# Sample attention of a decoder step: keys turned in 32x32 blocks on VectorE, scores on four row groups, new tokens once for all batches

## The chip, the cores and the metric

The kernel runs on one core of one Trainium2 chip. The metric is the device time of one launch in microseconds (us); lower is better. Profiles come from one execution that the hardware profiler recorded. Engine names are those of the profile: PE is TensorE, PEld its weight load, DVE VectorE, ACT ScalarE, POOL GpSimd, SP SyncE (here an issuer of DMAs).

## The reference

One step of a hybrid decoder layer in float32: 256 prompt tokens and 8 batches of 8 sample tokens go through two token mixers in parallel (HGRN2 with 8 heads, and MLA attention with 8 heads), a gated merge, an output projection and a squared-ReLU MLP, with modulated norms in between. The model width is 2048. The part that is changed is the sample attention:

```python
def mla_sample_attention(q_lat, q_pe, ckv_new, kpe_new, cache_ckv_l, cache_kpe_l, page_table):
    ckv_past = cache_ckv_l[page_table].reshape(Bd, -1, KV_RANK)      # 8 x 1024 x 512
    kpe_past = cache_kpe_l[page_table].reshape(Bd, -1, ROPE_DIM)     # 8 x 1024 x 64
    s_past = einsum('bthc,bsc->bhts', q_lat, ckv_past) + einsum('bthr,bsr->bhts', q_pe, kpe_past)
    s_new = einsum('bthc,bsc->bhts', q_lat, ckv_new) + einsum('bthr,bsr->bhts', q_pe, kpe_new)
    s_new = where(causal, s_new, -inf)
    p = softmax(concatenate([s_past, s_new], -1) * MLA_SCALE)
    return einsum('bhts,bsc->bthc', p[..., :P], ckv_past) + einsum('bhts,bsc->bthc', p[..., P:], ckv_new)
```

Per batch there are 64 queries (8 tokens of 8 heads) with 512 + 64 features, 1024 past tokens on 8 pages of a pool, and the 8 new tokens of the batch. The cached rows are both keys and values.

## The kernel before

Most of the program is large projections, features on partitions, 320 tokens (256 + 64) as the moving columns. `gemm` takes 256 columns of a weight matrix: SP loads 8 x 128 rows of it into a `raw` tile (pool `wraw`, three of 1 MB each); ACT casts half of a tile at a time to a rounded part `whi` and DVE subtracts it for a remainder `wlo` (pool `whl`, three of each); three PE products per block then give float32 accuracy (`whi` with the high part of the tokens, `whi` with the low, `wlo` with the high). PSUM has eight banks of 512 columns: four in pool `acc`, four in pool `aux`.

The MLA mixer projects two heads at a time (`mla_proj`), does the prompt's attention for them, and leaves the absorbed sample queries in `qst`: six blocks of 128 partitions, of which four are the 512 latent features and two hold the 64 rotary features on the lower and on the upper half of the partitions. A first projection for the other mixer, `early_proj(0)`, stands behind the last pair of heads, and `early_proj(1)` behind the sample attention.

The sample attention runs over the eight batches in turn. For each:

- `gather(b)` (L735) issues three indirect DMAs on POOL: the rotary keys `kraw` and the latent rows in two halves of 512 tokens, the first into `craw` (pool `sr`, three buffers), the second into a `raw` tile of `wraw`. A partition holds eight tokens.
- `past_scores(b, hf)` (L751), once for each half: PE turns 16 blocks of 128 x 128 through PSUM, which ACT and DVE copy by turns to `th` tiles; then products of 64 queries with 512 keys, the feature blocks by turns on two column groups of PE, accumulate in one bank; `kraw` is turned and multiplied in the same way. `fold` (L727) has ACT copy one column group to `Ss2` and DVE add it to the other.
- `new_scores(b)` (L782) adds the scores against the new tokens of all batches, with a mask that leaves those of batch b.
- `softmax` (L790), on DVE and ACT, over 64 x 1088 scores.
- `turn(b-1)` (L798) turns P on PE; `values(b-1)` (L808) multiplies it with `craws` and `ckvs` (the new tokens' rows) in eight products on two column groups and a ninth; `latent(b-2)` (L818) adds the column groups and turns the result into `olat`.

`at` says behind which feature block of `past_scores(b)` the steps of the batches before it are issued. The last batch's turn, values and latent are in `sample_tail` (L847), a generator which `gemm` advances between quarters of `early_proj(1)`'s products. What follows is the value projection with `w_kv_up` on `olat` (L859 to L870). Each engine works through its own queue in order; the queue's order is made from the program by the framework's scheduler, and tiles of a pool are given to a new user when the last reader of the old one is done.

Of the kernel before, what the change touches and what calls it, by code (L numbers as in the profile page):

```python
# [18 lines left out]
NP = 256  # L19
NB = 8  # L20
# [62 lines left out]
def tile_hgrn2_mla_step(  # L83
# [68 lines left out]
    def load_w(w2d, k0, nk, c0, ncols, src=None):  # L152
        """rows k0*128.., columns c0..: hi / lo operand views per k tile"""
# [39 lines left out]
    def gemm(w2d, kt0, nkt, c0, xh, xl, fine=False):  # L193
        """[256 columns of w2d from c0].T @ x -> two banks [128, N]"""
# [18 lines left out]
    def rstd_of(x, tmp, r):  # L213
        """r = 1/sqrt(x), x already mean square plus eps"""
# [32 lines left out]
    ckvs = keep.tile([NS, RANK], F32, name="ckvs")  # L247
    xsm = x_sample.rearrange("b t d -> (b t) d")
# [4 lines left out]
    qst = mq.tile([P, 6, NB, NS], F32, name="qst")  # L253
# [47 lines left out]
    def ada_turn():  # L301
        """the last columns of the conditioning, features on partitions, with their bias"""
# [10 lines left out]
    def ada_gen():  # L313
        """the conditioning, nb blocks of 128 columns of it (mod[:, b0:b0+nb, :]) in nb steps"""
# [70 lines left out]
    part1 = dram.tile([P, 4, 2, N], F32, name="part1")  # L385

# [1 line left out]
    def partial(f0, nf, cols, outs):  # L388
        """adds the rows of features f0.. of two 256-column blocks of w_in to outs"""
# [24 lines left out]
    def partial_kpe(f0, nf):  # L414
        """the rotary key's columns, on both partition halves"""
# [54 lines left out]
    def hg_gates(qT, qr, fg, fr, tmp, hp):  # L470
        """query and forget gates of a pair of heads"""
# [103 lines left out]
    nc.gpsimd.memset(qst[64:P, 4], 0.0)  # L575
    nc.gpsimd.memset(qst[0:64, 5], 0.0)

    def early_proj(j):
        """a projection of the second pair of heads, ahead of the mixer: forget (0) or query (1)"""
        ps = gemm(w_in, 0, KF, (1024, 0)[j] + 256, hh, hl, True)  # L580
        for h in range(2):
            nc.scalar.copy(out=part[:, 4 + j, h], in_=ps[h][:, 0:N])

    with mstack, pool("mp2", 2) as mp2:
        def mla_proj(i):
# [5 lines left out]
            # absorbed weights of the sample queries  # L591
# [6 lines left out]
            # queries  # L598
# [21 lines left out]
            # keys and values  # L620
# [24 lines left out]
            # sample queries: absorbed, and rotary on both partition halves  # L645
            for m in range(2):
# [8 lines left out]
                nc.scalar.copy(out=qst[64:P, 5, :, hs], in_=v)  # L655
# [40 lines left out]

        pend = None
        for i in range(NH // 2):
# [14 lines left out]
    # sample attention over the paged cache  # L713
    ostack = ExitStack()
    olp = ostack.enter_context(pool("olp"))
    olat = olp.tile([P, RF, NH, NS], F32, name="olat")
    ckv_rows = cache_ckv[0].rearrange("n (g j) c -> (n g) (j c)", j=8)
    kpe_rows = cache_kpe[0].rearrange("n (g j) c -> (n g) (j c)", j=8)
    with pool("sr", 3) as sr, pool("sc", 2) as sc, pool("s1") as s1:

        def cp(i, out, in_):
            if i % 2:
                nc.vector.tensor_copy(out=out, in_=in_)
            else:
                nc.scalar.copy(out=out, in_=in_)

        def fold(S, psc, cs, n, mask=None):  # L727
            """adds the two column groups of the scores"""
            S2 = s1.tile([NS, 512], F32, name="Ss2")
            nc.scalar.copy(out=S2[:, 0:n], in_=psc[64:P, 0:n])  # L730
            if mask is not None:
                add(S2[:, 0:n], S2[:, 0:n], mask)
            add(S[:, cs], psc[0:64, 0:n], S2[:, 0:n])

        def gather(b):  # L735
# [13 lines left out]
            return kraw, craws  # L749

        def past_scores(b, hf, S, kraw, craw, at):  # L751
            psc = bank(acc)
            ths = []

            def scores(f):
                for g in range(2):
                    mm(psc[64 * g:64 * (g + 1)], qst[:, f + g, b], ths[f + g], f == 0, False)

            for f in range(RF):
                pt = bank()  # L760
                for j in range(4):
                    transpose(pt[:, j * P:(j + 1) * P], craw[:, j, f * P:(f + 1) * P], P)
                th = sc.tile([P, 512], F32, name="th", bufs=4)
                cp(f, th, pt)
                ths.append(th)
                if f == 2:
                    scores(0)
                if f in at:
                    at[f]()
            pt = bank()  # L770
            for j in range(2):
                transpose(pt[:, j * P:(j + 1) * P],
                          kraw[:, 4 * hf + 2 * j:4 * hf + 2 * j + 2].rearrange("p o c -> p (o c)"), P)
            kt = sc.tile([P, 2, P], F32, name="ktp")
            cp(hf, kt, pt[:, 0:256].rearrange("p (j s) -> p j s", j=2))
            scores(2)
            pv_ = psc.rearrange("p (j o s) -> p o j s", j=2, o=2)
            for g in range(2):
                mm(pv_[64 * g:64 * (g + 1), g], qst[:, 4 + g, b], kt, False, True)
            fold(S, psc, slice(hf * 512, (hf + 1) * 512), 512)  # L780
# [619 lines left out]
```

## Time and profile before

| what | before |
|---|---|
| time, median of three runs | 2184.15 us (2177.47, 2185.85, 2184.15) |
| span of the profiled execution | 2179.5 us |
| PE busy | 2126.7 us, 98% |
| DVE busy | 1076.7 us, 49% |
| ACT busy | 877.8 us, 40% |
| POOL busy | 165.7 us, 8% |
| bytes moved by DMA | 401.94 MB, mean 184 GB/s |
| mean granted PE clock | 0.995 |

The profiled execution has no time of its own beside its span, which runs from the first to the last instruction. Busy shares are means over the span; the sample attention lies at about 375 to 532 us in it. In a row of a timeline the first number is the start, the second the duration, and what stands in brackets at its end is the time the engine was idle before it and what ended that. Rows of the same kind close together are one row with a count.

### The profile page before, as it was taken

How to read it: one execution, taken by the hardware profiler on the slowest of the kernel's cores; microseconds unless marked ns; L12 is line 12 of the kernel's file. 1: busy time of each engine (PE TensorE's matmuls, PEld its weight loads, DVE VectorE, ACT ScalarE, POOL GpSimd, SP SyncE). 2: the span in 40 equal slices, each digit the busy share in tenths (PEclk: the TensorE clock that was granted, in tenths of full speed). 3: DMA queues.
4: the chain of work that ended last, by engine and by line, in shares of the span. 5: the costliest groups of instructions: out<-in, count | busy, mean ns of one | idle time of the engine just before them, and what ended most of it. 6: DMA issues, size and time to landing. Idle time of an engine off the chain costs nothing.

```text
span 2179.5 us, 34849 instructions
## 1 busy us (share of the span) xinstructions
PE 2126.7 (98%) x14716; PEld 1908.5 (88%) x14716; DVE 1076.7 (49%) x1644; ACT 877.8 (40%) x1328; POOL 165.7 (8%) x158
## 2 busy tenths in 40 slices
PE   6999999999899999999999899999999999999997
PEld 3788988457688888999999599999999999999996
DVE  3556743443865646543443643344444444444455
ACT  4432443333554445333343543434333333333353
POOL 0000001110531311000010000000000000000001
PEclk9999999999999999999999999999999999999998
DMA  8986555235577668766864555545444544454442
GB/s 253 322 297 238 163 170 198 92 131 159 169 245 242 215 220 280 226 213 196 261 227 139 193 162 187 157 153 155 147 146 153 155 146 147 153 155 145 147 151 71
DMA packets 327571, 401.94 MB, mean 184 GB/s; under 512 B 10984, under 2 KB 265528, under 8 KB 324472
## 3 DMA queue, kind: packets, MB, share of 16 engines
q1 hardware_dynamic: 301576, 363.07, 51.8%
q0 software_dynamic: 3584, 21.50, 2.8%
q10 hardware_dynamic: 22256, 15.16, 2.3%
q8 instruction: 115, 1.88, 0.4%
q14 instruction: 40, 0.33, 0.0%
HBM read 387.69 MB, written 12.01 MB: 183 GB/s over the span
## 4 chain that ended last, share of the span: by engine, by line
PE 89%; issue 4%; DVE 3%; ACT 1%; DMA 1%; POOL 1%; SPq 0%; DVEq 0%; ACTq 0%; POOLq 0%
PE acc L131 77%; PE aux L131 8%; PE aux L134 4%; DVE wlo L143 1%; DMA raw<-in_w_in_dram 1%; POOL X L137 1%; ACT whi L146 1%; DMA xt<-in_x_sample_dram 0%; DVE zu L1363 0%; DVE x L1280 0%; DVE X L143 0%; DVE zg L137 0%; POOL qt L137 0%; DVE qn L494 0%; DVE bb L913 0%
## 5 line engine op out<-in xcount | busy, mean ns | idle before, releaser
L143 DVE TENSOR_TENSOR wlo<-raw,whi 128x1024 fp32r<-128x1024 f32 (+1 forms) x493 | 602.1, 1227 | 721.2 <-ACT whi L146 721.0
L146 ACT CAST whi<-raw 128x1024 fp32r<-128x1024 f32 (+1 forms) x493 | 501.6, 1025 | 809.2 <-PE acc L131 647.9
L131 PE MATMUL acc<-hh,whi 128*128 128x320 f32 x1168 | 369.0, 317 | 3.4 <-ACT hh L146 2.3
L131 PE MATMUL acc<-hl,whi 128*128 128x320 f32 x1168 | 361.8, 310 | 0.3 <-DVE hl L143 0.3
L131 PE MATMUL acc<-hh,wlo 128*128 128x320 f32 x1168 | 360.5, 311 | 0.0
L131 PE MATMUL acc<-uh,whi 128*128 128x320 f32 x1024 | 316.6, 309 | 0.0
L131 PE MATMUL acc<-gh,whi 128*128 128x320 f32 x1024 | 316.2, 309 | 0.0
L131 PE MATMUL acc<-gh,wlo 128*128 128x320 f32 x1024 | 316.1, 309 | 0.0
L131 PE MATMUL acc<-ul,whi 128*128 128x320 f32 x1024 | 316.1, 309 | 0.0
L131 PE MATMUL acc<-uh,wlo 128*128 128x320 f32 x1024 | 316.0, 309 | 0.0
L131 PE MATMUL acc<-gl,whi 128*128 128x320 f32 x1024 | 315.9, 309 | 0.0
L131 PEld LDWEIGHTS acc<-hh,whi 128*128 128x128 f32 x1168 | 219.6, 188 | 33.7 <-issue 18.2
L131 PEld LDWEIGHTS acc<-hl,whi 128*128 128x128 f32 x1168 | 219.6, 188 | 2.9 <-DVE hl L143 1.4
L131 PEld LDWEIGHTS acc<-hh,wlo 128*128 128x128 f32 x1168 | 218.9, 188 | 3.2 <-DVE wlo L143 2.5
L131 PEld LDWEIGHTS acc<-uh,whi 128*128 128x128 f32 x1024 | 192.5, 188 | 1.7 <-ACT u L1332 0.8
L131 PEld LDWEIGHTS acc<-gh,whi 128*128 128x128 f32 x1024 | 191.9, 187 | 1.8 <-ACT u L1333 0.8
L131 PEld LDWEIGHTS acc<-ul,whi 128*128 128x128 f32 x1024 | 192.4, 188 | 0.0
L131 PEld LDWEIGHTS acc<-uh,wlo 128*128 128x128 f32 x1024 | 192.4, 188 | 0.0
L131 PEld LDWEIGHTS acc<-gh,wlo 128*128 128x128 f32 x1024 | 192.0, 187 | 0.1
L131 PEld LDWEIGHTS acc<-gl,whi 128*128 128x128 f32 x1024 | 192.0, 188 | 0.0
L131 PE MATMUL aux<-raw,cT 128*32 128x512 f32 (+1 forms) x832 | 113.7, 593 | 16.7 <-DVE tt L137 11.9
L140 POOL TENSOR_TENSOR ssum<-ssum,sqt 128x320 f32<-128x320 f32 x26 | 25.9, 997 | 981.2 <-ACT sqt L1213 966.8
(409 smaller groups left out, 2602.2 us busy)
## 6 DMA issues: line engine op xcount, KB each, us to landing
raw<-in_w_ada_dram SPq DMA_DIRECT2D x96, 1024.0 KB, 6.9
raw<-in_w_up_dram SPq DMA_DIRECT2D x64, 1024.0 KB, 5.7
raw<-in_w_down_dram SPq DMA_DIRECT2D x64, 1024.0 KB, 5.8
raw<-in_w_in_dram SPq DMA_DIRECT2D x60, 1024.0 KB, 6.2
raw<-in_w_o_dram SPq DMA_DIRECT2D x16, 1024.0 KB, 5.9
raw<-in_w_in_dram SPq DMA_DIRECT2D x20, 512.0 KB, 6.4
raw<-in_w_b_out_dram SPq DMA_DIRECT2D x8, 1024.0 KB, 6.3
raw<-in_w_a_out_dram SPq DMA_DIRECT2D x8, 1024.0 KB, 5.8
```

Of the source, the lines that this page charges most:

```text
L131: nc.tensor.matmul(out, lhsT=lhsT, rhs=rhs, start=start, stop=stop)
L134: nc.tensor.transpose(out=out, in_=in_, identity=ident[:k, :k])
L137: (eng or nc.vector).tensor_tensor(out=out, in0=a, in1=b, op=ALU.mult)
L140: (eng or nc.vector).tensor_tensor(out=out, in0=a, in1=b, op=ALU.add)
L143: return (eng or nc.vector).tensor_tensor(out=out, in0=a, in1=b, op=ALU.subtract)
L146: nc.scalar.copy(out=hi, in_=src)
```

## The change

- The keys are turned by DVE. `blocks32` is one `nc.vector.transpose` over 128 x 512 elements, which turns each 32 x 32 block in its place. A batch takes eight of them into tiles of the pool `whl` (`th` is now a `whi` or a `wlo`) and one for the rotary keys, `ktp`.
- A block of 32 keys on 32 partitions of feature block k stays on its own partition group q. Scores are products of 32 rows, 64 queries and 256 keys: 18 feature blocks of 32 for each of four partition groups, by turns on two column groups. Each partition group has a PSUM bank of its own, so that a batch takes all four banks of `acc`. `fold` becomes four copies of 64 x 256 on ACT and four adds on DVE.
- The queries are needed on all four partition groups. `sample_queries` writes them to a DRAM tensor `qdr` with 18 DMAs issued on ACT, behind the last `mla_proj`; `gather` reads a batch's queries four times into `qrep` with DMAs on SP.
- The scores against the new tokens are computed in `sample_queries` for all batches, into `snew`; `softmax` has POOL copy them into S. The scale by the sum's reciprocal moves from DVE to ACT.
- P of the new tokens is collected in `pnew`; the product with `ckvs` is done once for all batches at the end (four products and four adds in `sample_tail`). The bank of `values` comes from `aux`.
- `qst` has five blocks, and its pool closes before the attention. Comments and docstrings are left out of the file.

```diff
+        def sample_queries():
+            for bc_ in range(4):
+                for f in range(RF):
+                    nc.scalar.dma_start(out=qdr[:, :, 4 * f + bc_].rearrange("b u q -> u b q"),
+                                        in_=qst[32 * bc_:32 * (bc_ + 1), f])
+            for k in range(2):
+                nc.scalar.dma_start(out=qdr[:, :, 16 + k].rearrange("b u q -> u b q"), in_=qst[32 * k:32 * (k + 1), 4])
+            for b in range(NB):
+                psn = bank()
+                for f in range(RF):
+                    g = f % 2
+                    mm(psn[64 * g:64 * (g + 1), 0:NS], qst[:, f, b], ckvT[:, f, NP:N], f < 2, f == 3)
+                mm(psn[0:64, 0:NS], qst[:, 4, b], kpeT[:, NP:N], False, True)
+                nc.scalar.copy(out=snew[:, b], in_=psn[64:P, 0:NS])
+                add(snew[:, b], snew[:, b], cst[0:NS, C_NEW + b * NS:C_NEW + (b + 1) * NS])
+                add(snew[:, b], psn[0:64, 0:NS], snew[:, b])
...
+        sample_queries()
         early_proj(0)
...
+            qrep = sc.tile([P, 18, NS], F32, name="qrep", bufs=3)
+            for q in range(4):
+                nc.sync.dma_start(out=qrep[32 * q:32 * (q + 1)], in_=qdr[b])
+            return kraw, craws, qrep
+        def blocks32(out, src):
+            nc.vector.transpose(out=out.rearrange("p k j u -> p j k u"),
+                                in_=src.rearrange("p j (k u) -> p j k u", u=32))
+        def turn_keys(b, kraw, craws):
+            ths = []
             for f in range(RF):
-                pt = bank()
-                for j in range(4):
-                    transpose(pt[:, j * P:(j + 1) * P], craw[:, j, f * P:(f + 1) * P], P)
-                th = sc.tile([P, 512], F32, name="th", bufs=4)
-                cp(f, th, pt)
+                th = whl.tile([P, 1024], F32, name="wlo" if f % 2 else "whi").rearrange(
+                    "p (k j u) -> p k j u", k=4, j=8)
+                for hf in range(2):
+                    blocks32(th[:, :, 4 * hf:4 * hf + 4], craws[hf][:, :, f * P:(f + 1) * P])
                 ths.append(th)
+            kt = sc.tile([P, 2, 8, 32], F32, name="ktp")
+            blocks32(kt, kraw)
+            return ths, kt
+        def past_scores(b, S, ths, kt, qrep):
+            psc = [bank(acc) for _ in range(4)]
+            for k0 in range(0, 18, 2):
+                for q in range(4):
+                    qs = slice(32 * q, 32 * (q + 1))
+                    for g in range(2):
+                        k = k0 + g
+                        rhs = (ths[k // 4][qs, k % 4] if k < 16 else kt[qs, g]).rearrange("p j u -> p (j u)")
+                        mm(psc[q][64 * g:64 * (g + 1), 0:256], qrep[qs, k], rhs, k0 == 0, k0 == 16)
+            Sv = S[:, 0:PAST].rearrange("t (j q u) -> t q j u", j=8, q=4)
+            for q in range(4):
+                S2 = s1.tile([NS, 256], F32, name="Ss2", bufs=2)
+                nc.scalar.copy(out=S2, in_=psc[q][64:P, 0:256])
+                add(Sv[:, q], psc[q][0:64, 0:256].rearrange("t (j u) -> t j u", j=8),
+                    S2.rearrange("t (j u) -> t j u", j=8))
+        def softmax(b, S):
             mx = sc.tile([NS, 2], F32, name="mxs")
+            nc.gpsimd.tensor_copy(out=S[:, PAST:PAST + NS], in_=snew[:, b])
...
-            nc.vector.tensor_scalar(out=S, in0=S, scalar1=mx[:, 1:2], scalar2=None, op0=ALU.mult)
+            nc.scalar.activation(out=S, in_=S, func=AF.Copy, scale=mx[:, 1:2])
...
-            nc.vector.tensor_copy(out=PT[0:64, 8], in_=pt2[0:64, 0:64])
+            nc.vector.tensor_copy(out=pnew[:, b], in_=pt2[0:64, 0:64])
...
         def values(PT, craws):
-            po = bank(acc)
+            po = bank()
...
-            mm(po[0:64], PT[0:64, 8], ckvs, False, True)
...
         for b in range(NB):
+            kraw, craws, qrep = gather(b)
             S = sc.tile([NS, PAST + NS], F32, name="Ss")
+            ths, kt = turn_keys(b, kraw, craws)
+            past_scores(b, S, ths, kt, qrep)
+            if b > 1:
+                latent(b - 2, ot)
+            if b:
+                PT = turn(b - 1, st["S"])
+            softmax(b, S)
+            if b:
+                ot = values(PT, st["c"])
+            st["S"], st["c"] = S, craws
...
             latent(NB - 1, ot)
+            for f in range(RF):
+                pn = pns[f % 2]
+                mm(pn, ckvs[:, f * P:(f + 1) * P], pnew.rearrange("s b q -> s (b q)"), True, True)
+                ov = olat[:, f].rearrange("p h (b t) -> p b h t", t=NT)
+                add(ov, ov, pn.rearrange("p (b h t) -> p b h t", b=NB, h=NH))
```

The order of the instructions on the engines moves with it. The rows below are from the engines' queues; a number behind a name is that of the tile, and the last figures are the shape. First DVE in the middle of the attention, before the change: `th` and `ktp` are copies of turned keys, `Ss` the scores and `mxs` the softmax's maximum and sum.

```order
L795 RECIPROCAL mxs_3836<-mxs_3836 64x1
L796 TENSOR_SCALAR Ss_3713<-Ss_3713,mxs_3836 64x1088
L140 TENSOR_TENSOR Ss_3848<-acc_3849,Ss2_3895 64x512
L723 COPY th_3921<-aux_3916 128x512
L140 TENSOR_TENSOR Ss2_3904<-Ss2_3904,cst_75 64x64
L805 COPY PTs_3934<-aux_3924 64x64
L140 TENSOR_TENSOR Ss_3848<-acc_3898,Ss2_3904 64x64
L723 COPY th_3951<-aux_3946 128x512
L723 COPY ktp_3968<-aux_3965 128x256
L140 TENSOR_TENSOR Ss_3848<-acc_3908,Ss2_3974 64x512
L723 COPY th_4003<-aux_3998 128x512
L792 TENSOR_REDUCE mxs_3977<-Ss_3848 64x1
```

And the same stretch of DVE's queue now, from one batch's reciprocal on (`craw_4256` and `raw_4258` hold the keys of the batch after the one whose scores are `Ss_4113`):

```order
L803 RECIPROCAL mxs_4084<-mxs_4084 64x1
L764 STREAM_TRANSPOSE whi_4266<-craw_4256 128x4x4x32
L764 STREAM_TRANSPOSE wlo_4269<-craw_4256 128x4x4x32
L764 STREAM_TRANSPOSE whi_4272<-craw_4256 128x4x4x32
L764 STREAM_TRANSPOSE whi_4266<-raw_4258 128x4x4x32
L764 STREAM_TRANSPOSE wlo_4269<-raw_4258 128x4x4x32
L764 STREAM_TRANSPOSE whi_4272<-raw_4258 128x4x4x32
L764 STREAM_TRANSPOSE wlo_4275<-craw_4256 128x4x4x32
L764 STREAM_TRANSPOSE wlo_4275<-raw_4258 128x4x4x32
L140 TENSOR_TENSOR Ss_4113<-acc_4128,Ss2_4204 64x8x32
L140 TENSOR_TENSOR Ss_4113<-acc_4129,Ss2_4207 64x8x32
L140 TENSOR_TENSOR Ss_4113<-acc_4130,Ss2_4210 64x8x32
```

The eight turns of the next batch's keys now stand ahead of the adds of this batch's scores. On PE, at the same place, from the latent step of the batch before last (`Ss_4113` and `craw_4104` are of one batch, `whi_4418` and `qrep_4412` of the next but one):

```order
L131 MATMUL aux_4368<-cst_75,ot_4252 128x64 x4
L134 MATMUL aux_4374<-ident_76,Ss_4113 128x64 x8
L134 MATMUL aux_4375<-ident_76,Ss_4113 64x64
L131 MATMUL acc_4432<-whi_4418,qrep_4412 64x256 x2
L131 MATMUL acc_4433<-whi_4418,qrep_4412 64x256
L131 MATMUL aux_4395<-craw_4104,PTs_4385 64x512 x4
L131 MATMUL aux_4395<-raw_4106,PTs_4385 64x512 x4
L131 MATMUL acc_4433<-whi_4418,qrep_4412 64x256
```

Three score products of the batch after the next stand between the turn of a batch's P and its values. On ACT, ahead of the attention (`Sp`, `mxp`: the last prompt softmax; `whi_3551` and what follows it: `early_proj(0)`), before:

```order
L673 ACTIVATE Sp_3424,mxp_3427<-Sp_3424,mxp_3427 128x128
L675 ACTIVATE Sp_3424,mxp_3427<-Sp_3424,mxp_3427 128x256
L146 CAST whi_3526<-raw_3496 128x1024
L582 COPY part_86<-acc_3436 128x320
L582 COPY part_86<-acc_3437 128x320
```

and now:

```order
L673 ACTIVATE Sp_3417,mxp_3420<-Sp_3417,mxp_3420 128x128
L675 ACTIVATE Sp_3417,mxp_3420<-Sp_3417,mxp_3420 128x256
L701 DMA qdr_164<-qst_102 32x8x64 x11
L711 COPY snew_98<-aux_3447 64x64
L711 COPY snew_98<-aux_3456 64x64
L711 COPY snew_98<-aux_3465 64x64
L146 CAST whi_3551<-raw_3521 128x1024
L146 CAST whi_3581<-raw_3579 128x1024
L711 COPY snew_98<-aux_3474 64x64
L146 CAST whi_3609<-raw_3579 128x1024
```

Eleven DMA issues and three copies stand between the last prompt softmax and the casts of `early_proj(0)`.

More of the change, by code (lines that the diff above doesn't have):

```diff
@@ L711, in tile_hgrn2_mla_step @@
     lrstack.close()
+    qst_stack.close()
     ostack = ExitStack()
@@ L770, in past_scores @@
[L770 to L779, printed above, removed]
@@ L780, in past_scores @@
-            fold(S, psc, slice(hf * 512, (hf + 1) * 512), 512)
-        def new_scores(b, S):
-            psn = bank(acc)
-            for f in range(RF):
-                g = f % 2
-                mm(psn[64 * g:64 * (g + 1), 0:NS], qst[:, f, b], ckvT[:, f, NP:N], f < 2, f == 3)
-            mm(psn[0:64, 0:NS], qst[:, 4, b], kpeT[:, NP:N], False, True)
-            fold(S, psn, slice(PAST, PAST + NS), NS, cst[0:NS, C_NEW + b * NS:C_NEW + (b + 1) * NS])
-        def softmax(S):
+                th = whl.tile([P, 1024], F32, name="wlo" if f % 2 else "whi").rearrange(
+                    "p (k j u) -> p k j u", k=4, j=8)
```

58 lines of the change are left out of this document (12 added, 46 removed).

## The prediction

> **What bounds the kernel now.** I read the page's head first, then the windows around the sample attention, then single engines' timelines inside one batch of it.
>
> ```profile
> span 2179.5 us, 34849 instructions
> PE 2126.7 (98%) x14716; PEld 1908.5 (88%) x14716; DVE 1076.7 (49%) x1644; ACT 877.8 (40%) x1328; POOL 165.7 (8%) x158
> PE 89%; issue 4%; DVE 3%; ACT 1%; DMA 1%; POOL 1%; SPq 0%; DVEq 0%; ACTq 0%; POOLq 0%
> ```
>
> TensorE (PE) is busy 98% of the span and carries 89% of the chain that ended last. Whatever takes work off it shortens the program, unless something else then makes it wait. The windows give the stage that is changed and one batch of it (columns: PE, weight loads, DVE, ACT, POOL busy, granted clock, DMA share, GB/s):
>
> ```profile
> 374.00:532.00 158.00, 157.56 (x940) 86.84 (x941) 66.08 (x127) 57.68 (x103) 15.09 (x16) 1.00 0.36 118
> 430.00:447.70 17.70, 17.70 (x108) 9.01 (x106) 7.28 (x16) 6.46 (x12) 2.83 (x3) 1.00 0.40 134
> ```
>
> PE never idles here; DVE works 7.28 of 17.70 us. Two gathers of the POOL timeline give the period of a batch, 454.21 - 436.50 = 17.71 us, and show that a gather starts when a values product of PE lets its buffer go:
>
> ```profile
> 436.50 0.94 POOL L747 DMA_INDIRECT craw<-in_cache_ckv_dram,pidx  x1 [12.44 <-PE acc L131]
> 440.83 0.94 POOL L747 DMA_INDIRECT raw<-in_cache_ckv_dram,pidx  x1 [0.30 <-issue]
> 454.21 0.94 POOL L747 DMA_INDIRECT craw<-in_cache_ckv_dram,pidx  x1 [12.44 <-PE acc L131]
> ```
>
> Nobody waits for that gather now: its keys are wanted a whole batch later. From the PE timeline (an f32 product is two records; products in two column groups overlap):
>
> ```profile
> 434.28 1.94 PE L131 MATMUL acc<-craw,PTs 128*64 128x512 f32 x8
> 436.05 1.89 PE L131 MATMUL acc<-raw,PTs 128*64 128x512 f32 x8
> 437.87 1.07 PE L131 MATMUL acc<-ckvs,PTs 64*64 64x512 f32 x2
> 438.87 0.44 PE L134 MATMUL aux<-ident,kraw 128*128 128x128 f32 x2
> 439.24 1.08 PE L131 MATMUL acc<-th,qst 128*64 128x512 f32 x4
> 440.14 0.60 PE L131 MATMUL acc<-ktp,qst 128*64 128x256 f32 x4
> 440.68 1.09 PE L134 MATMUL aux<-ident,craw 128*128 128x128 f32 x8
> ```
>
> Values of one batch take 437.87 - 434.28 = 3.59 us, the new tokens' product on one column group 1.00, two score products of 512 columns 440.14 - 439.24 = .90. The stage runs from 374.97 to the first product of `olat`, 532.41: 157.4 us.
>
> ```profile
> 374.97 1.47 PE L134 MATMUL aux<-ident,craw 128*128 128x128 f32 x12
> 532.41 1.78 PE L131 MATMUL aux<-olat,raw 128*128 128x64 f32 x15
> ```
>
> **The change, part by part.**
>
> *PE loses work.* The 40 transposes of a batch, the new tokens' scores and the ckvs product go; 72 products of 32 rows and 256 columns replace 18 of 512. No row shows 32-row groups at work. By the .90 above a column pair of 256 costs .45, so 36 pairs cost 16.2 us if the four row groups run in turn and 4.05 if they run together. I take 4.05: each group has its own rows, its own bank and its own queries. With .7 for turning P, 1.0 for `latent` and 3.59 for values PE then needs about 9.4 us a batch where it needs 17.7: at most 8.3 us a batch to win.
>
> *DVE gains nine turns of 512 columns a batch*, and loses its half of the PSUM copies.
>
> ```profile
> 426.97 0.69 DVE L723 COPY th<-aux 128x512 f32<-128x512 f32 x1 [0.41 <-PE aux L134]
> 429.93 0.68 DVE L140 TENSOR_TENSOR Ss<-acc,Ss 64x512 f32<-64x512 f32 x1 [0.18 <-ACT Ss L730]
> 424.90 1.27 DVE L792 TENSOR_REDUCE mxs<-Ss 64x1 f32<-64x1088 f32 x1
> L143 DVE TENSOR_TENSOR kt<-bb 128x512 f32<-128x512 f32 x4 | 4.9, 1225 | 0.1
> ```
>
> A turn moves as much as the copy (.69); the dearest 512-column row is 1.225. Bounds .55 (a fifth under the copy) to 1.225; I take .70, since a turn reads one operand as the copy does. DVE's sum: 9 x .70, four adds of 256 columns at .40 (.68 halved, and something for the fixed part), reduce 1.27, small ones .9: 10.1 us a batch.
>
> [...]
>
> *A chain forms.* In DVE's order the eight turns of batch b+2 stand ahead of the adds of batch b+1. On PE three score products stand ahead of `values(b)`, and they need banks that the first two of those adds free. `values(b)` frees the buffers that gather b+3 waits for. So each period is: half of values, gather, last turns, two adds, three products, and round again; what was hidden under 17.7 us of PE work is now in series.
>
> ```profile
> raw<-in_w_in_dram SPq DMA_DIRECT2D x60, 1024.0 KB, 6.2
> raw<-in_cache_ckv_dram,pidx POOLq DMA_INDIRECT x8, 5.8
> craw<-in_cache_ckv_dram,pidx POOLq DMA_INDIRECT x8, 8.1
> ```
>
> Landings: 5.8 us for the gather of `raw` (1 MB), and 10.1 from the issue of `craw` to the landing of `raw` in the timeline above (440.83 - 436.50 + 5.8), with 4.3 of it between the issues. Issued one behind the other I estimate 5.5 for `craw` and 3.2 more for `raw` (8.7; bounds 5.8 and 10.1). Three turns fit into the 3.2; five follow. Period: 1.9 + 5.5 + 3.2 + 5 x .70 + 2 x .40 + .4 + about .7 of hand-overs = 16.0 us, against 17.71.
>
> *The clock.* PE then works 9.4 of 16 us, with its idle time in one piece of 5 to 6. What follows such a piece is seen elsewhere in this trace (clock is the third number from the end):
>
> ```profile
> 1222.00:1225.50 3.50, 1.69 (x16) 0.16 (x8) 3.46 (x7) 1.75 (x3) 0.00 (x0) 1.00 1.04 403
> 1225.50:1228.90 3.40, 1.14 (x12) 0.16 (x8) 3.40 (x4) 3.27 (x7) 0.00 (x0) 1.00 1.05 408
> 1228.90:1232.30 3.40, 1.93 (x8) 0.20 (x8) 1.57 (x6) 2.85 (x7) 0.00 (x0) 0.50 1.05 408
> 1232.30:1235.80 3.50, 3.48 (x14) 1.21 (x14) 3.44 (x15) 0.00 (x0) 0.00 (x0) 0.51 1.05 409
> ```
>
> A window with PE at 1.14 of 3.40 is followed by 3.4 us and more at .50. Here the products that come next are those on the chain, .4 + 1.9 us; at half clock they cost up to 2.3 more, and since the phase wanders I take 1.3: a period of 17.3.
>
> *Ahead of the stage.* Eighteen DMA issues on ACT write the queries out, eleven of them in a row, ahead of the copies of the new scores and of `early_proj(0)`'s casts.
>
> ```profile
> 259.28 0.54 ACTq L514 DMA_DIRECT2D out_dram<-ckvs  x1
> 259.88 0.56 ACTq L521 DMA_DIRECT2D out_dram<-ktok  x1
> 260.49 1.20 ACTq L522 DMA_DIRECT2D out_dram<-ktok  x1
> 360.00 1.04 ACT L146 CAST whi<-raw 128x1024 fp32r<-128x1024 f32 x1
> 370.12 0.31 PE L131 MATMUL acc<-hh,wlo 128*128 128x320 f32 x1
> ```
>
> At .54 to .6 an issue, 11 take some 6 us from 360.0 on, where ACT now casts; PE stands meanwhile, and 4 us of new-score products move here as well. I add 10.1 (bounds 4 and 13). Of the moved DMAs the 32 loads of `qrep` stand on SP between the two projections' weight loads; they are due a batch ahead and hidden as long as the gather is what is waited for.
>
> *The tail.* ACT and DVE have the hi and lo parts of `early_proj(1)`'s first weights ahead of the last batch's adds. Its second load waits for a lo part of the first, and the first for `values(5)`.
>
> ```profile
> 491.11 10.06 SPq L156 DMA_DIRECT2D raw<-in_w_in_dram  x2
> 507.11 1.23 DVE L143 TENSOR_TENSOR wlo<-raw,whi 128x1024 fp32r<-128x1024 f32 x1 [1.78 <-ACT whi L146]
> 512.27 0.67 DVE L140 TENSOR_TENSOR Ss<-acc,Ss 64x512 f32<-64x512 f32 x1
> ```
>
> Today's issue of the second load waits too (10.06 us) but PE has scores to do. Then: `values(5)` 3.9, load 5.8 to 6.2, cast 1.04, two lo parts 2.4, second load 6.2, cast and lo 2.3: the adds come some 7 us after their place in the period. Behind them:
>
> ```profile
> 427.46 1.20 ACT L794 ACTIVATE Ss<-Ss,mxs 64x1088 f32<-64x1088 f32 x1
> 428.56 0.19 ACT L794 ACTIVATION_READ_ACCUMULATOR Ss<-Ss,mxs 64x1 f32 x1
> 369.97 0.31 PE L131 MATMUL acc<-hl,whi 128*128 128x320 f32 x1
> ```
>
> 9.7 us to the end of the last turn (two adds .8, reduce 1.3, exponential 1.4, the scale, now on ACT over the same 1088 columns, 1.2, turn .7; the rest hand-overs, and PE on GEMM products in between), 4.4 to the values (copy of P, and a quarter of the GEMM: 24 products at 370.12 - 369.97 = .15 are 3.6), values 3.8, another quarter 3.6, `latent` 1.0, four new-token products of 512 columns 3.5, the last quarter 3.6: 29.6, and 29.8 with the hand-overs.
>
> **The sum**, in us after PE is free: adds of batches 0, 1 and 2 at 8.3, 15.3 and 31.4 (their keys have landed; DVE's twelve queued turns set the pace, then the chain); four periods of 16.0 to batch 6 at 95.5; the last adds at 95.5 + 16 + 7.5 = 119.0; end at 148.8. With the half clock: 32.5, four of 17.4 to 102.1, 126.5, end 158.6. Against 157.4 and with 10.1 ahead: +1.5 at full clock, +11.3 with the clock halved each period. I take the second, 2179.5 + 11.3 = 2190.8 for the profiled execution; on the median of the runs, 2184.15 + 11.3 = 2195.5. The profiled span lies 4.65 below that median, inside the spread 2177.47 to 2185.85. What this measurement tells from no change is about 0.5%, 10.9 us.
>
> **The rivals.**
> 1. *The chain binds, the clock holds*: +1.5, 2186. For it: windows at half load (1.69 of 3.50) are not followed by .50 above. Against: the idle piece is longer than a window.
> 2. *The gather runs ahead*, landing faster or being released earlier than I read, so that DVE's 10.1 us (with hand-overs 10.6) sets the period: (17.7 - 10.6) x 6.5 = 46 less, + 10 ahead = -36, 2148; a gather of 6 instead of 8.7 alone gives 2.7 x 7 = 19 less than my sum, 2176. For it: 118 GB/s in the stage against 403 to 409 above, so the DMAs have room. Against: one gather's own 5.8.
> [...]
> 4. *Row groups run in turn*: 16.2 + 5.3 = 21.5 us a batch on PE, 3.8 x 8 = 30 over before, and the 10 ahead and the tail's 6: 2230. For it: no row shows four groups together. Against: column pairs do overlap (two products of 512 columns in .90, one alone in 1.00).
>
> **How the numbers follow.** Main case .45: its own range, with hand-overs, phase and the ACT issues at their bounds, is 2185 to 2210, so .17 of it lies within 0.5% and .28 above. Rival 1 .18, all within. Rival 2 .20, faster. Rival 3 .09 and rival 4 .08, slower. Faster .20, same .35, slower .45. The range 2168 to 2228 leaves out the far part of rival 2 (about .12) and rival 4 with the end of 3 (.07).
>
> **What would show it.** In the changed trace: STREAM_TRANSPOSE rows of about .70; POOL's gathers 17 us apart, their wait ending on a `values` product of PE; DVE's turns waiting for DMA `raw`; PE idle 5 to 6 us a batch ahead of score products, released by DVE's adds; clock near .8 in the stage; eleven ACT issues and PE idle by 361 to 367; DVE's lo parts ahead of the last adds. The forecast is wrong if the turns wait for nothing, if PE has no long idle piece, if the four row groups' products start more than .1 us apart in a row, or if a turn is far from .70.

## The result and the profile after

The changed kernel takes 2207.07 us (median of four runs, 2205.07 to 2212.29) against 2183.64 us before (2177.47 to 2185.85): ratio 1.0104, 95% interval 1.0086 to 1.0121. It is slower by 23 us. The forecast was slower by 11.3, 2195.5, with a range of 2168 to 2228.

The head of the page after, and the line on which source lines carry the chain that ended last:

```profile
span 2206.2 us, 36328 instructions
PE 2098.0 (95%) x15380; PEld 1901.5 (86%) x15380; DVE 1098.7 (50%) x1688; ACT 866.0 (39%) x1304; POOL 168.1 (8%) x165
PE acc L131 74%; PE aux L131 10%; PE aux L134 2%; DMA raw<-in_cache_ckv_dram,pidx 2%; DMA raw<-in_w_in_dram 2%; DVE wlo L143 1%; ACT whi L146 1%; POOL X L137 1%; DVE wlo L764 0%; DVE whi L764 0%; DMA xt<-in_x_prompt_dram 0%; DVE zu L1370 0%; DVE x L1287 0%; DMA oB<-obs 0%; DVE X L143 0%
```

PE is busy for 28.7 us less and the program still got longer: the gather of `raw`, which nobody waited for, now stands on the chain with 2%, and the load of `in_w_in` with 2% instead of 1%. Three rows of PE's timeline give the borders of the stage, the first score product and the first product of `olat`, and the wait ahead of it:

```profile
367.43 0.70 PE L131 MATMUL aux<-ckvT,qst 128*64 128x64 f32 x8 [6.79 <-DVE snew L140]
386.02 1.14 PE L131 MATMUL acc<-whi,qrep 32*64 32x256 f32 x20
554.51 7.25 PE L131 MATMUL aux<-olat,raw 128*128 128x64 f32 x64
```

The stage starts 386.02 - 374.97 = 11.05 us later and takes 554.51 - 386.02 = 168.5 us instead of 157.4: 22.1 us in all. The profiled spans differ by 26.7; the 4.6 us behind the stage are no part of the change (in the profiles below, that rest of the program varies between 1647 and 1655 us).

Four periods in the windows view (columns as before: PE, PEld, DVE, ACT, POOL busy, granted clock, DMA share, GB/s):

```profile
407.00:427.40 20.40, 12.00 (x175) 6.80 (x175) 9.06 (x19) 5.30 (x11) 2.42 (x4) 0.75 0.49 146
427.40:447.80 20.40, 12.67 (x179) 6.93 (x177) 8.90 (x18) 5.00 (x10) 3.03 (x5) 0.75 0.48 146
447.80:468.20 20.40, 12.93 (x179) 6.98 (x177) 8.91 (x18) 5.23 (x10) 2.19 (x4) 0.75 0.42 133
468.20:486.70 18.50, 12.86 (x177) 6.90 (x175) 8.91 (x18) 5.03 (x10) 2.12 (x4) 0.76 0.34 115
```

No engine is busy for more than 13 of 20.4 us, where PE was busy for all of its 17.7 before; the work is in series. The clock is granted at .75. The ring can be read off three timelines. POOL's gathers, released by a values product:

```profile
427.11 0.97 POOL L755 DMA_INDIRECT craw<-in_cache_ckv_dram,pidx  x1 [2.28 <-PE aux L131]
428.83 0.94 POOL L755 DMA_INDIRECT raw<-in_cache_ckv_dram,pidx  x1 [0.75 <-PE aux L131]
...
447.58 0.97 POOL L755 DMA_INDIRECT craw<-in_cache_ckv_dram,pidx  x1 [2.30 <-PE aux L131]
```

DVE's turns, released by the landings, with the adds behind them:

```profile
433.08 0.71 DVE L764 STREAM_TRANSPOSE whi<-craw 128x512 f32<-128x512 f32 x1 [6.01 <-DMA craw<-in_cache_ckv_dram,pidx]
...
438.90 0.71 DVE L764 STREAM_TRANSPOSE whi<-raw 128x512 f32<-128x512 f32 x1 [3.92 <-DMA raw<-in_cache_ckv_dram,pidx]
...
441.91 0.71 DVE L140 TENSOR_TENSOR Ss<-acc,Ss 64x256 f32<-64x256 f32 x2
```

And PE's three products (six records) with the values behind them, released by the adds:

```profile
442.34 1.44 PE L131 MATMUL acc<-whi,qrep 32*64 32x256 f32 x6 [7.64 <-DVE Ss L140]
443.74 3.55 PE L131 MATMUL aux<-craw,PTs 128*64 128x512 f32 x8
447.12 1.88 PE L131 MATMUL aux<-raw,PTs 128*64 128x512 f32 x8
```

From gather to gather: `craw` lands 6.0 us behind its issue (427.11 to 433.08), `raw` another 5.8 later, turns 3.0, adds .4, three products 1.4, half of the values 3.4 where they took 1.8 before, and the next gather at 447.58: 20.5 us.

### The profile page after: what moved, and what is told of

Same layout as the page of the kernel before. It is cut to its first block, busy times and chain, and to the rows that moved or that the text cites. A ratio compares the mean times of both kernels' runs of the same rounds, so it can differ in the third digit from the quotient of the medians.

```text
span 2206.2 us, 36328 instructions
## 1 busy us (share of the span) xinstructions
PE 2098.0 (95%) x15380; PEld 1901.5 (86%) x15380; DVE 1098.7 (50%) x1688; ACT 866.0 (39%) x1304; POOL 168.1 (8%) x165
## 4 chain that ended last, share of the span: by engine, by line
PE 86%; DVE 5%; DMA 4%; issue 2%; ACT 2%; POOL 1%; ACTq 0%; SPq 0%; DVEq 0%; POOLq 0%
PE acc L131 74%; PE aux L131 10%; PE aux L134 2%; DMA raw<-in_cache_ckv_dram,pidx 2%; DMA raw<-in_w_in_dram 2%; DVE wlo L143 1%; ACT whi L146 1%; POOL X L137 1%; DVE wlo L764 0%; DVE whi L764 0%; DMA xt<-in_x_prompt_dram 0%; DVE zu L1370 0%; DVE x L1287 0%; DMA oB<-obs 0%; DVE X L143 0%
## 5 line engine op out<-in xcount | busy, mean ns | idle before, releaser
L131 PE MATMUL acc<-hh,whi 128*128 128x320 f32 x1168 | 370.5, 318 | 14.9 <-DVE Ss L140 11.5
L131 PEld LDWEIGHTS acc<-hh,whi 128*128 128x128 f32 x1168 | 220.2, 189 | 46.8 <-issue 19.3
```

The source lines that it names most:

```text
L131: nc.tensor.matmul(out, lhsT=lhsT, rhs=rhs, start=start, stop=stop)
```

## The experiments

Each kernel was timed against the kernel before on the same chip; its ratio stands beside the changed kernel's 1.0104. One per cent is 22 us. Code is cut down to the lines that matter, and comments in it are added here. Where a place in the profile is compared, it is the first product of `olat`, at 554.51 in the changed kernel.

### One ordering edge on TensorE

```diff
+            with behind(st.get("v")):          # the last product of values(b-2)
                 past_scores(b, S, ths, kt, qrep)
```

(`behind` queues what the block issues on an engine behind the instruction named.)

> The changed kernel with one ordering edge on TensorE: the score products of batch b+2 are queued behind the values of batch b, instead of three of them ahead. Nothing else is changed. Theory (series): values wait for DVE's adds through those three products, the adds for turns, the turns for a gather, the gather for values; 20.4 us a batch. Without the three products values(b) wait only for the softmax of b. The ring then goes over two batches: 1.9 + gather 10 + turns 3.5 + adds 1.7 + softmax 4.5 + turn of P and copy 1.4 = 23, 11.5 a batch; five to six periods shorter by 8.5 to 8.9: about 2207 - 46 = 2161, and under the kernel before. Rival (transfers): the gather and the loads of the queries share the DMA engines and set the pace, whatever the order on PE: some 2 us a batch from the earlier start, 2195. Rival (DVE): nine turns on DVE set the pace: no change, 2207.

Measured: 1.0124 (1.0094 to 1.0153): no change. The number is that of the rival on DVE, for another reason, as the run with DVE's order changed shows below. What falls is the reading that the three products alone hold the values. PE's queue, then ACT's, of this kernel say what holds them:

```profile
442.18 3.68 PE L131 MATMUL aux<-craw,PTs 128*64 128x512 f32 x8 [9.33 <-ACT PTs L817]
```

```profile
440.82 0.70 ACT L798 COPY Ss<-acc 64x256 f32<-64x256 f32 x2 [9.06 <-DVE Ss L143]
441.55 0.58 ACT L817 COPY PTs<-aux 128x512 f32<-128x512 f32 x1
```

The copy of P, `PTs`, is queued on ACT behind the third and fourth copies of the next batch's scores, and these wait 9 us for a `Ss2` buffer that DVE's adds give back. There were two links in parallel from the adds to the values, one on PE and one on ACT.

### The other link, and both

```diff
-                S2 = s1.tile([NS, 256], F32, name="Ss2", bufs=2)
+                S2 = s1.tile([NS, 256], F32, name="Ss2", bufs=4)
```

This edit alone, with TensorE's order as it was:

> The changed kernel with four Ss2 buffers instead of two, and TensorE's order as it is (three score products ahead of the values). Theory (two parallel links, each enough): the link on TensorE holds the values as before: no change, 2207 (within 6). If the link on ACT alone were what counts, it would be 2164.

Measured: 1.0095 (1.0070 to 1.0120): no change, as the theory of two links has it. In its profile `PTs` is copied at 432.95 and the values still start only at 441.14, behind three products that wait 6.80 us for an add. And with the edge on TensorE beside it:

> The changed kernel with values ahead of the score products on TensorE, and with four Ss2 buffers instead of two. The second edit is for the second link that the trace of the first showed: on ACT the copies 3 and 4 of the scores wait for a Ss2 buffer that DVE's adds free, and the copy PTs, which the values wait for, is queued behind them. With both links out, values(b) wait only for the softmax of b. Theory (series, two parallel links): the ring goes over two batches, by rows of the changed kernel: values .. gather's landing .. turns .. adds 16.7, softmax, turn of P and copy 8.5: 25 for two, 12.6 a batch instead of 20.4; five to six periods: 2207 - 43 = 2164, under the kernel before. Rival (transfers): gathers and query loads set the pace: not under 2190. Rival (DVE's order, turns ahead of adds, is itself the bound): 2205.

Measured: 1.0022 (1.0009 to 1.0036), some 18 us shorter than the changed kernel; the first product of `olat` is at 539.6. So each link alone holds the values, and it takes both edits to gain. But 43 us were expected. PE's timeline shows what still waits:

```profile
440.43 3.12 PE L131 MATMUL acc<-whi,qrep 32*64 32x256 f32 x30 [3.28 <-DVE Ss L143]
...
448.00 1.10 PE L131 MATMUL aux<-cst,ot 128*128 128x64 f32 x8
449.03 0.77 PE L134 MATMUL aux<-ident,Ss 64*128 64x64 f32 x9
450.42 1.94 PE L131 MATMUL aux<-craw,PTs 128*64 128x512 f32 x8 [0.62 <-ACT PTs L817]
```

The whole score products of the next batch wait for banks that the adds free, and the turn of P and the values are queued behind them: a third way from the adds to the values, longer by one batch's scores. That this third way is what the missing 25 us are is read from the queue; the next run tests it only by cutting all three ways at once.

### The turns behind the adds

All three ways begin at adds that stand behind turns. One edge on DVE takes that away (TensorE's order moves with it, the values ahead of the score products, which alone had gained nothing):

```diff
+            with behind(st.get("a")):          # the last add of batch b-1
                 ths, kt = turn_keys(b, kraw, craws)
```

> The changed kernel with one ordering edge on DVE: the turns of batch b+1 are queued behind the adds of batch b. (TensorE's order moves with it: the values come ahead of the score products.) Theory: the adds wait for no gather any more, so neither link matters; what is left is the reciprocal of b behind four turns of b+1, a ring of 18.7 over two batches, and DVE's own 10.1 and waits of one batch: 11 to 12.6 a batch, 2155 to 2165. Rival (transfers): not under 2190. Rival (turns cost what they cost, DVE sets the pace wherever they stand): 2205.

Measured: 0.9886 (0.9867 to 0.9904): 2160 us, inside the theory's 2155 to 2165 and under the kernel before. Two of POOL's gathers, the longest wait of DVE's turns, and the windows from these gathers to the next:

```profile
427.12 0.96 POOL L760 DMA_INDIRECT craw<-in_cache_ckv_dram,pidx  x1 [2.61 <-PE aux L131]
439.29 0.97 POOL L760 DMA_INDIRECT craw<-in_cache_ckv_dram,pidx  x1 [2.61 <-PE aux L131]
```

```profile
428.65 0.71 DVE L769 STREAM_TRANSPOSE whi<-raw 128x512 f32<-128x512 f32 x1 [1.87 <-DMA raw<-in_cache_ckv_dram,pidx]
```

```profile
427.10:439.30 12.20, 10.34 (x181) 5.65 (x179) 9.07 (x19) 4.92 (x10) 3.10 (x5) 1.00 0.85 258
439.30:449.50 10.20, 9.43 (x180) 5.91 (x178) 8.29 (x18) 4.86 (x10) 3.08 (x4) 1.00 0.65 232
```

Periods are 10.2 to 12.2 us. PE is busy for 9.4 of the shortest and DVE for 8.3: their work now lies side by side, with PE the busier, and the gather is waited for by at most 1.9 us. The nine turns as such weren't what made the change slow: there are as many of them here.

### The loads of the queries

```diff
-            for q in range(4):
-                nc.sync.dma_start(out=qrep[32 * q:32 * (q + 1)], in_=qdr[b])
+            if b < 3:      # loaded for three batches, used for all
...
```

> The changed kernel without the loads of qrep for batches 3 to 7, which use the queries of batches 0 to 2 instead (their results are those of other queries). Theory: in the periods with these loads raw lands 5.8 us behind craw, in the last, without them, 3.9 to 2.9; they cost the chain about 2 us a batch in four periods: 8 us, 2199. Rival (the gather's own packets are what takes the time): no change, 2207.

Measured: 1.0055 (1.0038 to 1.0073), 11 us shorter (8 expected). The gathers:

```profile
424.02 0.97 POOL L757 DMA_INDIRECT craw<-in_cache_ckv_dram,pidx  x1 [1.98 <-PE aux L131]
442.85 0.97 POOL L757 DMA_INDIRECT craw<-in_cache_ckv_dram,pidx  x1 [2.42 <-PE aux L131]
461.45 0.97 POOL L757 DMA_INDIRECT craw<-in_cache_ckv_dram,pidx  x1 [10.43 <-PE aux L131]
```

18.8 and 18.6 us apart instead of 20.5 and 20.3, and 19.2 instead of 21.1 in the period before: the loads cost the chain 1.6 to 2.0 us in each of these three periods. The fourth, in which the changed kernel has no such loads either, is 19.3 instead of 18.5, and the first product of `olat` comes 3.8 us earlier. The rest of the 11 us is not explained by the gathers.

Windows between the issue of a gather and the landing of its second half show what the DMAs do, first in the changed kernel (427.11 to 438.90), then in this one (442.85 to 452.98):

```profile
429.30:437.00 7.70, 5.31 (x139) 4.22 (x123) 1.90 (x3) 0.67 (x2) 0.47 (x1) 0.99 0.93 312
437.00:438.90 1.90, 0.00 (x0) 0.00 (x0) 0.00 (x0) 0.00 (x0) 0.00 (x0) 0.50 0.35 75
```

```profile
444.40:450.50 6.10, 6.10 (x159) 4.78 (x155) 1.84 (x3) 1.29 (x3) 0.94 (x1) 1.00 0.93 336
450.50:452.98 2.48, 0.15 (x3) 0.00 (x0) 0.06 (x2) 0.00 (x0) 0.23 (x1) 1.00 0.07 26
```

For 7.7 us of the one and 6.1 us of the other the DMAs are 93% busy, at 312 and 336 GB/s. At the end of both stand some 2 us in which little moves, and the turns wait for their end too.

### The clock

```diff
+            with behind(last):                 # the last product of the turn of P
+                for _ in range(nf):
+                    st["f"] = mm(pt2[0:64, 64:512], ident[:, 0:64], cst[:, 0:448], True, True)
...
```

(The lines left out keep the order of all else on TensorE.)

> The changed kernel with products of no use (64 x 448, into unused columns of a bank) on TensorE behind the turn of P of batches 1 to 5 (6, 6, 6, 4 and 2 of them), where TensorE idles 8.3 to 3.6 us; the order of all else is the same. Theory: the idle piece halves the clock of the three score products and of the first values, which cost 1.44 and 3.4 us where .5 and 1.8 would do: 2.4 us a batch on the chain, five times: 12 us, 2195. If the clock is not granted by how busy TensorE was, or if the half clock is off the chain: 2207.

Measured: 1.0070 (1.0045 to 1.0095), some 7 us shorter, 12 expected. In PE's timeline the filling was too short in two periods of the first three; here are the first two, and the fourth:

```profile
420.65 1.44 PE L131 MATMUL acc<-whi,qrep 32*64 32x256 f32 x6 [4.33 <-DVE Ss L143]
422.05 3.68 PE L131 MATMUL aux<-craw,PTs 128*64 128x512 f32 x8
...
439.96 1.94 PE L131 MATMUL aux<-craw,PTs 128*64 128x512 f32 x8 [0.43 <-ACT PTs L825]
...
476.93 0.97 PE L131 MATMUL acc<-whi,qrep 32*64 32x256 f32 x6 [1.60 <-DVE Ss L143]
478.33 3.13 PE L131 MATMUL aux<-craw,PTs 128*64 128x512 f32 x8 [0.43 <-ACT PTs L825]
```

After an idle piece of 4.3 us, and of 4.8 in the third period, the first half of the values takes 3.68 us, in the period without one 1.94. In the fourth it takes 3.13 although the pieces ahead of it are only 1.60 and .43 us. So it was filled longer:

> The changed kernel with more products of no use behind the turn of P of batches 1 to 5 (10, 10, 9, 6 and 3 instead of 6, 6, 6, 4 and 2); the order of all else is that of the changed kernel. With six of them TensorE still idled 4.3 to 4.8 us in two of four periods and ran the products behind at half speed there; in the period without such an idle piece the values took 1.94 + 1.89 us and the gathers stood 16.2 us apart. Theory (the half clock costs some 2.4 us a period): no idle piece over 2 us is left, the clock in the periods is over .95, and the time is 2207 - 12 = 2195 (2190 to 2200). If the clock is full and the periods still are 20 us, the half clock is off the chain, and the gathers alone set it: 2205.

Measured: 1.0085 (1.0054 to 1.0116), which can't be told from the shorter filling, nor safely from the changed kernel. Two windows of this kernel:

```profile
407.00:427.40 20.40, 19.98 (x245) 9.79 (x247) 9.05 (x19) 6.90 (x12) 4.63 (x6) 1.00 0.55 165
...
468.20:486.70 18.50, 17.21 (x228) 9.43 (x213) 10.06 (x20) 5.64 (x11) 2.13 (x3) 1.00 0.43 153
```

The full clock is there, and the gathers stand 18.1, 18.8, 19.8 and 16.4 us apart, mean 18.3 against 20.1 in the changed kernel: 1.85 us a period, 7 in the four, and the first product of `olat` is 5.2 us earlier. From the first of the three products to the next gather it is 3.3 to 3.6 us here and 5.2 to 5.4 in the changed kernel, so that the gain lies where the half clock was. So the half clock is on the chain, at some 1.8 us a period; what the timed runs show of it, some 4 to 7 us, is near their uncertainty. What idle time halves the clock stays open: idle pieces of 4.3 us and more are followed by products of double length (3.68 us for the first half of the values), and one of 2.03 us in the longer filling is not (1.94 us); but behind the 1.60 and .43 us above the two halves of the values take 3.13 and 2.44 us, where they take 1.94 and 1.89 at full clock, so that these runs give no threshold.

### The stores of the queries

```diff
-                    nc.scalar.dma_start(out=qdr[:, :, 4 * f + bc_] ...
+                    nc.sync.dma_start(out=qdr[:, :, 4 * f + bc_] ...
```

(and the same for the two stores of the rotary part)

> The changed kernel with the 18 stores of the queries issued on SP instead of ACT. Theory: the eleven issues in a row on ACT (.47 each, 361.4 to 366.5) hold back the copies of the new scores, and PE idles 6.79 us for them: 6 us shorter, 2201, unless SP's weight loads for the projection behind now come late by the same. Rival: the 11 us that the stage starts later are the new-score products themselves: no change, 2207.

Measured: 1.0048 (1.0027 to 1.0070), 12 us shorter; in the profile the stage starts with this row of PE:

```profile
378.69 1.14 PE L131 MATMUL acc<-whi,qrep 32*64 32x256 f32 x20
```

7.3 us earlier than 386.02. What is left of the later start is 3.7 us. The new-score products would account for it: in the kernel that has this part of the change alone (below) they stand ahead of the stage for 4.0 us, 373.31 to 377.30.

### The tail

```diff
-        early_proj(1)
+        with behind(st["a"]), behind(st["c2"]):     # the last add on DVE, the last copy of scores on ACT
+            early_proj(1)
```

> The changed kernel with the casts and lo parts of the projection behind the attention queued behind the last batch's copies and adds, and nothing else. Theory: the adds of the last batch stand at 523.2 us in the changed kernel, 25 us behind those of the batch before, where a period is 18.5 to 20.4; TensorE idles 11.5 us for them. 6 us shorter: 2201. If the loads set the end in any case: 2207.

Measured: 1.0028 (1.0009 to 1.0046), 17 us shorter where 6 were expected. DVE's adds of the last two batches in the changed kernel, and then in this one:

```profile
498.18 0.71 DVE L140 TENSOR_TENSOR Ss<-acc,Ss 64x256 f32<-64x256 f32 x2
...
522.05 1.23 DVE L143 TENSOR_TENSOR wlo<-raw,whi 128x1024 fp32r<-128x1024 f32 x1 [6.66 <-ACT whi L146]
523.19 0.74 DVE L140 TENSOR_TENSOR Ss<-acc,Ss 64x256 f32<-64x256 f32 x2
```

```profile
495.07 0.71 DVE L143 TENSOR_TENSOR Ss<-acc,Ss 64x256 f32<-64x256 f32 x2
...
507.68 0.74 DVE L143 TENSOR_TENSOR Ss<-acc,Ss 64x256 f32<-64x256 f32 x2 [7.30 <-ACT Ss L798]
```

The last adds came 25.0 us behind those before them, and now come 12.6 behind: 12.4 us. I had set the lateness against a period of 18 to 20, but the last batch has no turns ahead of its adds, and needs no period of that length.

### One part of the change alone

The kernel before with the new tokens computed once for all batches, and the keys turned on TensorE as ever:

```diff
-            new_scores(b, S)
...
+        sample_queries()        # the scores of the new tokens, all batches, into snew
...
-            mm(po[0:64], PT[0:64, 8], ckvs, False, True)
...
+                mm(pn, ckvs[:, f * P:(f + 1) * P], pnew.rearrange("s b q -> s (b q)"), True, True)
```

> The kernel before with one part of the change alone: the scores of the new tokens are computed once for all batches ahead of the attention, their product with ckvs once at the end, and the keys are turned on TensorE as before. Theory: TensorE is the bound there, so what it loses counts: per batch the product with ckvs, 1.0, the turn of the new part stays; the scores of the new tokens cost the same once as eight times (5 products for each batch either way); the four products at the end cost 3.9: 8 x 1.0 - 3.9 = 4 less, 2180 (2176 to 2186). So this part isn't what makes the change slower; if it comes out over 2195, it is.

Measured: 1.0022 (1.0006 to 1.0039): no gain, and at most a small loss. POOL's gathers and the row of the products at the end:

```profile
437.91 0.97 POOL L749 DMA_INDIRECT craw<-in_cache_ckv_dram,pidx  x1 [5.04 <-PE acc L131]
454.94 0.97 POOL L749 DMA_INDIRECT craw<-in_cache_ckv_dram,pidx  x1 [5.04 <-PE acc L131]
```

```profile
525.95 3.88 PE L131 MATMUL aux<-pnew,ckvs 64*128 64x512 f32 x8
```

The period is 17.03 instead of 17.71: .68 a batch, 5.4 in eight, of which 3.9 go at the end. What I took as equal, the new tokens' scores, isn't quite: among other products they overlapped with those (in the kernel before the row of `ckvT` at 445.70, .28 us long, lies inside that of `th` at 444.80, 1.28 us long), and ahead of the stage they stand alone. Most of the slowness of the change isn't in this part: the interval leaves it 1 to 9 of the 23 us.

### Towards a faster kernel

The edge on DVE, with the stores on SP:

> The kernel with turns behind the adds, and with the 18 stores of the queries issued on SP. Theory: the start of the stage and its period are separate terms; the stores gave 7.5 us of the profile's span alone and give the same here: 2160 - 7.5 = 2152. If the earlier start only makes the first gathers wait longer, no gain: 2160.

Measured: 0.9851 (0.9825 to 0.9878): 2154.6 us against 2187.85 before on that chip. With the tail's edges as well:

> The same, and the casts and lo parts of the projection behind the attention queued behind the last batch's copies and adds, on ACT and on DVE. Theory: in the kernel with turns behind the adds TensorE idles 11.1 us ahead of the last adds, because the lo parts ahead of them wait for two weight loads one after the other; the adds wait for a gather or nothing when the lo parts stand behind. 7 us shorter, since the loads still have to come: 2145. If the projection's own products then wait for the loads instead, the stall moves on and nothing is gained: 2152.

Measured: 0.9785 (0.9759 to 0.9811): 2141.6 against 2187.85, 2.15% faster than the kernel before. The first product of `olat` is at 494.78, 59.7 us earlier than in the changed kernel and 37.6 earlier than before. Its windows over the middle of the attention:

```profile
407.00:427.40 20.40, 17.66 (x295) 9.88 (x279) 14.30 (x32) 8.11 (x16) 4.70 (x7) 1.00 0.84 269
427.40:447.80 20.40, 18.08 (x348) 11.16 (x350) 15.66 (x35) 8.48 (x17) 5.19 (x7) 1.00 0.77 262
```

PE is busy for 88% and DVE for 73% of the time, at full clock: the work that the change moved to DVE now lies beside PE's. Of the 70 us between 1.0104 and 0.9785 the edge on DVE brought 48, the stores 8 and the tail 14; on the changed kernel alone the stores had brought 12 and the tail 17.

## Why the prediction came out as it did

The sign and the chain were right, the size was half. In us of the profile, stage against the sum of the forecast (counted from the first score product):

| | forecast | measured |
|---|---|---|
| later start | 10.1 | 11.05 |
| adds of batch 2 | 32.5 | 35.4 |
| four periods | 4 x 17.4 | 4 x 19.2 |
| last adds behind those of batch 6 | 24.4 | 25.0 |
| from there to `olat` | 32.1 | 31.3 |
| total against before | +11.3 | +22.1 |

- **The turn**: .70 was taken. The group row says

```profile
L764 DVE STREAM_TRANSPOSE whi<-craw 128x512 f32<-128x512 f32 x16 | 11.1, 695 | 34.4 <-DMA craw<-in_cache_ckv_dram,pidx 28.1 <-PE acc L131 6.3
```

  .695, and in a row they start .60 apart; the five groups of turns lie between .671 and .695. No run shows a turn of over .71, so that the .09 for rival 3 (a dearer turn) and its part of the range have nothing measured under them.
- **Row groups** (rival 4): in the changed kernel's period the 69 products behind the first three take 4.4 us at full clock (428.47 to 432.90), .064 us from product to product. In the kernel with turns behind the adds all 72 stand together, between these two rows of PE:

```profile
440.66 1.12 PE L131 MATMUL acc<-whi,qrep 32*64 32x256 f32 x32
444.73 1.10 PE L131 MATMUL aux<-cst,ot 128*128 128x64 f32 x8
```

  4.07 us, against the 4.05 for all four groups together. Rival 4 falls.
- **The chain**: it closes as forecast, through gather, turns, adds and values, and moving the turns behind the adds removes it. Incomplete was the link from adds to values: I had only the three products on PE. The copy `PTs` behind two waiting copies on ACT does the same, and was to be seen in ACT's order. For the time of the change that made no difference; it decided which edits help.
- **The step that failed** is the size of "5.5 for `craw` and 3.2 more for `raw` (8.7; bounds 5.8 and 10.1)". `craw` took 5.6 to 6.0 us, near its term. `raw` took 6.8, 5.8 and 5.9 more in the three gathers with loads of `qrep` beside them, 12.5, 11.8 and 11.5 us in all, outside the bounds; in the last two, without such loads, 3.9 and 2.9, 9.7 and 8.7 in all. The four gathers of the four periods in the table are together 7.0 us over the 8.7, and the periods 7.1 over the forecast. With it falls "they are due a batch ahead and hidden as long as the gather is what is waited for" on the loads of `qrep`: they are in time themselves, but they move 144 KB four times while the gather is under way, the DMAs are 93% busy for 7.7 of its 11.8 us, and the gather is what is waited for. Without them the periods that had them are 1.6 to 2.0 us shorter. That `raw` still lands 10.0 to 10.8 us behind the issue of `craw` in that kernel stays open; the windows show an end of some 2 us in which little moves, and no run shows why.
- **Luck**: the rest of a period agrees with the forecast only in its sum. From 427.11 to 447.58 the three products and half of the values took 4.8 us where 3.6 were forecast with the clock's 1.3, the turns 3.0 for 3.5, the adds .4 for .8, hand-overs .5 for .7.
- **The half clock**: 1.3 us a period were taken, 1.6 to 1.9 measured by filling PE's idle time. That the phase wanders was my estimate, and no run shows it: in all four periods of the changed kernel the first half of the values takes 3.54 to 3.68 us, about double the 1.94. Rival 1 (the clock holds) falls by the .75 in the windows.
- **The start**: 10.1 against 11.05; of it 7.3 are the ACT issues, and the other 3.7 fit the moved products. Issues were put at .54 to .6 each, and took .47 (median).
- **Rival 2** (the gather runs ahead) is what one edge on DVE's queue makes true, though PE's work, not DVE's, fills most of the period then. Its ground, 118 GB/s as a mean over the stage, does not show room: in the changed kernel the DMAs are 93% busy for 7.7 of a gather's 11.8 us. The forecast's 36 us less for it were 24 less in the run, since the late start and the tail remained.

## What to carry to other kernels

When work moves from the busiest engine to an idle one, ask for the ring that it closes: here a buffer's release, a gather, the work on the moved keys and the release again, each of them cheap and none of them beside the other. Read each engine's queue for what stands behind the waiting instruction, and for all parallel ways round, before cutting one of them; cutting the common root (turns ahead of adds) gained 48 us where cutting one way gained nothing. And a transfer that is itself in time may still slow the one that is waited for, as the loads of the queries did here by 1.6 to 2.0 us a period.

## What the runs showed that was not expected

Two gathers of 1 MB, issued 1.7 us apart, landed 6.0 and 11.8 us after the first issue. The mean of 146 GB/s over the period looks like idle DMAs, but they are 48% busy over the period and 93%, at 312 GB/s, for 7.7 us of the gather; four loads of 144 KB beside it account for 1.6 to 2.0 us. Why a gather ends with some 2 us in which little moves isn't settled. And products of no use in TensorE's idle time, which only add work, raised the granted clock from .75 to 1.00 and brought the first half of the values on the chain back from 3.5 to 1.94 us.
